# A four-layer hybrid trunk: HGRN2's first two decay levels in one tiled series, attention's value products for two blocks at a time, queries turned two heads at once

## The chip, the cores and the metric

The kernel runs on one core of one Trainium2 chip. The metric is the device time of one execution in microseconds, given as the median of several runs. The engines are named as the profile names them: PE (matrix products), PEld (its weight loads), DVE (vector engine), ACT (scalar engine), POOL, and SP (which here only issues transfers).

## The reference, cut to what matters

Four layers over 1024 positions of width 1024, all in float32. Layers 0 and 3 are HGRN2, layer 1 is sliding-window attention, layer 2 is gated DeltaNet. Each layer normalizes x, applies a shift and scale from the conditioning, projects, mixes over time, projects back and adds to x under a gate. The change touches the mixing of the HGRN2 layers and of the attention layer:

```python
def step(S, inp):                       # HGRN2, per chunk of 64 and per head; d = 128
    q_, k_, v_, lf = inp
    b = jnp.cumsum(lf, axis=-2)
    diff = b[..., :, None, :] - b[..., None, :, :]
    dec = jnp.exp(jnp.where(causal[:, :, None], diff, -jnp.inf))
    A = jnp.einsum('bhtd,bhsd,bhtsd->bhts', q_, k_, dec)
    o = jnp.einsum('bhts,bhse->bhte', A, v_) + jnp.einsum('bhtd,bhde->bhte', q_ * jnp.exp(b), S)
    ...
# attention: 16 query heads of 64 in 4 groups, 4 key heads, blocks of 128 queries, window 128
s = jnp.einsum('bnqhgd,bnkhd->bnhgqk', qb, kb) * (SW_DH ** -0.5)      # 128 queries x 256 keys
m = jnp.maximum(jnp.max(s, axis=-1, keepdims=True), sink)
p = jnp.exp(s - m)
p = p / (jnp.sum(p, axis=-1, keepdims=True) + jnp.exp(sink - m))
o = jnp.einsum('bnhgqk,bnkhd->bnqhgd', p, vb)
```

The HGRN2 matrix A has a different decay for each of the 128 channels, so it isn't one matrix product of q and k: the decays have to be multiplied into q and k relative to some position that lies between them.

## The kernel before

Activations lie with features on partitions and tokens in the free dimension, in two halves of 512 tokens (`hf`). Every projection is done in split float32: each operand is a high and a low part, and `mm3` (lines 354 to 359) issues three matmuls of 128x512 per 128 input features (high·high, high·low, low·high). Weights come by DMA as `w_raw`, and ACT and DVE split them into `w_hi` and `w_lo` (lines 328, 329, and 331, 332 with a scale). A projection's result lies in one of three PSUM banks (`proj_ps`) until ACT and DVE have evacuated it.

A layer's work is written as generators that yield after each piece of matmul work. `weave` runs several of them side by side: in a head of HGRN2 the mixing of head h (`mix`), the projections of head h+1, and a side stream that prepares the next layer's modulation. The final order of the instructions in each engine's queue is not left to that: the table `ORDER` holds for each of PE, ACT, DVE, SP and POOL a compressed list of places, and `in_order` (line 165) ties every instruction to the one before it in that list. The lists come from a planner that ran ahead of time. An engine works through its queue strictly in that order.

**HGRN2 mixing** (`hgrn2`, from line 1156; `mix` from line 1245), per layer, head and half, which makes 2 x 8 x 2 = 32 units. A is built in levels of growing distance, in groups of 4 sub-blocks of j = 2, 8 and 32 tokens (l = 1, 3, 5); level 0 (neighbours) is done beside level 1 with operands that the evacuation of the projection made (`q` of 48 columns a group, `k0`). At each level, ACT copies and DVE products build `X`, the decayed queries (lines 1281 to 1283). Then `products` (lines 1254 to 1263) multiplies `X` with `kg`, the decayed keys: 16 small matmuls, each with a stationary operand of 128x32 and a moving one of 128x48, four side by side in the four column groups of the array, so that outputs land in 32-partition strips of a `lev_ps` bank. A float32 product is two instructions in the profile. `tied` (line 284) makes such a set one unbroken series in PE's queue. At level 1 the series has two operand pairs, `(X, kg)` and `(q, k0)`; at level 3 one. DVE writes the wanted entries into `A` with masked copies (lines 1290 to 1296), and then q, k and the decays F are scaled for the next level (lines 1315 to 1321; line 1319 overwrites `kg`). Level 5 has 16 products of another shape (line 1305). Then `kg` is turned (line 1327, `kh_ps`), and the outputs and states follow chunk by chunk (lines 1337 to 1350). Buffers of a tag are reused in turn; `bufs` (line 1164) gives their number.

**Attention mixing** (`swa`, from line 1496; `mix` from line 1605), per group of 4 query heads and block of 128 queries: 4 x 8 = 32 blocks. Four transposes of 64 columns turn the queries (line 1616, `qt_ps`), two ACT casts write the high part to both halves of `qhi` (lines 1619, 1620), one DVE subtraction the low part (line 1621). Per head, a band mask and two products give the scores `s_ps` (lines 1631 to 1633). After the softmax, probabilities are turned (line 1654), and line 1660 multiplies them with the values: 128x64 stationary, 128x256 moving, two side by side in the two column halves of the array, for each of the two key blocks (only one for the first block of the sequence), as one tied series. Line 1666 multiplies the result by the gate.

The output projection of HGRN2 reads the mixed heads 0 to 6 back from DRAM (`out_load`, line 1450, issued on POOL's queue) into three buffers of a pool of their own (lines 1409, 1410, 1416). `rope_tables` (line 489) makes the rotary tables during the first layer.

Of the kernel before, what the change touches and what calls it, by code (L numbers as in the profile page):

```python
# [34 lines left out]
SB = {"q": 2, "tmp": 4, "qhi": 2, "pth": 2, "sm": 2, "zs": 2, "of": 3}  # L35
# [16 lines left out]
        "c-rk->2n;#6@S{DJ!ZAit|VJ4OSaH`?dm=)S+<3YkYfWfKCz7xCm2i;QjnqwaHyErmJdv>0-N9jVoX&a<f0Oj4<-pDA5ul7@*$O~<XgVvU&w"  # L52
        "dzj-J_`-r1d9A4!qQuSzq$-90ni@4bHS_3Nils1Q(v0768;0tE{prQBkUuo;m9m>VEWF_H-CF*`f!6!m-Ux>_nG5b1OxMdfHTYDK8vei&d4q"
        "7MNcMDxJGVFixXgKiz~1b{pJ!hk%Auj=S{*FXmW+Mx~Zf>zi7>!AgjVI4FzK?WLOEv$hCsP_)&6nq0-fRk{hsj2B)6O_c0a7&o=t(^#f({IK"
        "=O$}ByHg*9tH!GGKklHZ>-8a!?D_3Q+;MN2KSqWg<c&V>1>w%E~<a=&3Q24HK1FCu%z7YWD1*-<k58Q>I`*Q{cxpgW}G#?yAXg^~yyrk2@k%"
        "v{~BZZG`62d<Oe=G&_sj;!^*ROwM0OsehX=%yr^}d1p^Zy7y!7%@7KyUlAf#Sk&0-l3spXDMJoI1wy!J_mvc^+;LlqA;y(BhFrFjS;3FRx~^"
        "Rur(s1^x|p5LE_Lb((?d*X)nFpJzx<wgvz@g%LddFjVp4_97Avd)^*5;1~(Iv&Dcq5S?FdP>Vqp0oXc)LgiDft*y<hN~eqT^>1*gg~*tVF@j"
        "71hrTWVRY)?jY$2juRJ}P5Y8HY*wE=Kz>CQH_!5mAqNiNrrmPxj70DJ^l^C=v1`M%n69SjjdYkdGhp@dp))waFXfbsIA0Tw6(IHJ@DLbr_HQ"
        "WR?4glPE-R}ld!DOQb*g^DH`Ws6A*!h&!-9!ds4oVgILpRi0KVD<YfeoK8Zf?NuPB0`&(E=pdRvJ?@Gx0FH<NrfOy43YyV;B^BFekz4J166D"
        "ls*n(^!%*S3OMOStEWfr`{C^YxTm!xW@?8V|-~74(_|L=f_anA#<NWLD>Rf7j;qZb4hvX%kLPTl>Ncb8uZ%n+9Qs%BulnZ@a4Gp(AuZf6>P7"  # L60
        "{%ih#&lxiVtpPRKprnmA2neeq)P|1xl2F>iWq)t3LTxmE+Qm+&NU@9YtLSm65zt5F0^X@)g=V@(M5Qs^LOo;q^&MsE|hx?vKZwQ8iB@zJ&;K"
# [1740 lines left out]
```

## Time and profile before

| | |
|---|---|
| median of 3 runs | 2592.4 us (2590.6 to 2597.68) |
| profiled execution | 2594.64 us, span 2592.9 us |
| mean granted TensorE clock | 0.991 |
| PE busy | 2538.1 us, 98% of the span, 18271 matmuls |
| PEld busy | 2061.2 us, 79% |
| DVE busy | 2044.0 us, 79% |
| ACT busy | 1328.4 us, 51% |
| POOL busy | 158.9 us, 6% |
| DMA | 312.06 MB in 393618 packets, mean 120 GB/s |

The first HGRN2 layer lies at about 60 to 600 us of the span, attention up to about 1060, DeltaNet up to about 2060, the second HGRN2 layer behind it. In rows of the profile "128\*32" behind a matmul means 128 rows and 32 columns of the array; the tile sizes after it are those of the moving operand or of the result; "x64" counts instructions. A matmul's own length overlaps with the next matmul's: what a matmul takes from the queue is the distance between the starts.

### The profile page before, as it was taken

To read this page: it belongs to the slowest core of one execution; us is meant where nothing else is said; L and a number is where in the kernel's file an instruction comes from. 1 tells how busy PE (TensorE), PEld (TensorE's weight loads), DVE (VectorE), ACT (ScalarE), POOL (GpSimd) and SP (SyncE) were. 2 spreads that over 40 slices of the span, in tenths; PEclk is the share of its full clock that TensorE was granted. 3 is DMA by queue.
4 is the path that set the end of the run, shared out by engine and by line. 5 is a ranking of instruction groups with operands and counts; after the bars stand their busy time and mean duration, and the time that the engine had idled before them with its cause. 6 is when DMAs were issued, how large, how long until landed. Compare 5 with 4: busy or idle time off the path is not lost.

```text
span 2592.9 us, 50817 instructions
## 1 busy us (share of the span) xinstructions
PE 2538.1 (98%) x18271; PEld 2061.2 (79%) x18271; DVE 2044.0 (79%) x5663; ACT 1328.4 (51%) x3480; POOL 158.9 (6%) x382
## 2 busy tenths in 40 slices
PE   8999999999999999999999999999999999999999
PEld 4777777788888867787887788788788878888887
DVE  6586788887788888778998999898777847478885
ACT  5344344543465656455666666666544534344452
POOL 0000000001000000100001101110212000000000
PEclk9999999999999999999999999999999999999999
DMA  8233443644233253434344344333576412122453
GB/s 292 85 115 83 143 135 119 192 130 151 58 94 98 87 162 103 140 107 113 96 123 114 87 124 117 82 95 90 179 229 206 130 30 89 55 86 67 129 160 119
DMA packets 393618, 312.06 MB, mean 120 GB/s; under 512 B 74980, under 2 KB 320151, under 8 KB 393367
## 3 DMA queue, kind: packets, MB, share of 16 engines
q1 hardware_dynamic: 380822, 267.92, 35.5%
q0 software_dynamic: 12544, 40.90, 4.9%
q8 instruction: 144, 2.36, 0.4%
q14 instruction: 108, 0.88, 0.1%
HBM read 247.84 MB, written 60.88 MB: 119 GB/s over the span
## 4 chain that ended last, share of the span: by engine, by line
PE 83%; DMA 7%; DVE 4%; ACT 2%; issue 1%; SPq 1%; POOL 0%; DVEq 0%; ACTq 0%; POOLq 0%
PE proj_ps L357 12%; PE proj_ps L358 12%; PE proj_ps L359 12%; PE outp_ps L358 5%; PE outp_ps L359 5%; PE outp_ps L357 5%; PE projw_ps L358 2%; PE projw_ps L357 2%; PE projw_ps L359 2%; PE projt_ps L358 2%; PE projt_ps L357 2%; DMA ada_w<-in_ada_w_dram 2%; PE projt_ps L359 2%; PE lev_ps L1260 2%; DMA w_raw<-in_hg_in_w_dram 1%
## 5 line engine op out<-in xcount | busy, mean ns | idle before, releaser
L357 PE MATMUL proj_ps<-hhi,w_hi 128*128 128x512 f32 x1664 | 677.6, 408 | 3.1 <-ACT gd_tb L831 2.9
L358 PE MATMUL proj_ps<-hlo,w_hi 128*128 128x512 f32 x1664 | 675.6, 406 | 0.0
L359 PE MATMUL proj_ps<-hhi,w_lo 128*128 128x512 f32 x1664 | 672.6, 405 | 0.0
L357 PEld LDWEIGHTS proj_ps<-hhi,w_hi 128*128 128x128 f32 x1664 | 315.3, 190 | 62.7 <-ACT gd_tb L831 4.9
L359 PEld LDWEIGHTS proj_ps<-hhi,w_lo 128*128 128x128 f32 x1664 | 315.1, 189 | 58.1 <-issue 1.5
L358 PEld LDWEIGHTS proj_ps<-hlo,w_hi 128*128 128x128 f32 x1664 | 315.5, 190 | 56.3 <-issue 1.3
L328 ACT CAST w_hi<-w_raw 128x512 fp32r<-128x512 f32 x356 | 216.5, 610 | 233.3 <-PE proj_ps L358 109.7
L329 DVE TENSOR_TENSOR w_lo<-w_raw,w_hi 128x512 fp32r<-128x512 f32 x356 | 237.9, 674 | 99.6 <-ACT w_hi L328 97.5
L358 PE MATMUL outp_ps<-o_lo,w_hi 128*128 128x512 f32 x576 | 229.0, 398 | 0.7 <-DVE o_lo L1466 0.7
L357 PE MATMUL outp_ps<-o_hi,w_hi 128*128 128x512 f32 x576 | 228.0, 398 | 0.0
L359 PE MATMUL outp_ps<-o_hi,w_lo 128*128 128x512 f32 x576 | 227.7, 396 | 0.0
L331 ACT ACTIVATE w_hi<-w_raw,par 128x512 fp32r<-128x512 f32 (+1 forms) x136 | 94.7, 698 | 132.2 <-PE outp_ps L358 76.4
L833 DVE SCALAR_TENSOR_TENSOR gd_tb<-gd_xs,taps,gd_tb 128x512 f32<-128x512 f32 x192 | 145.2, 756 | 10.2 <-ACT gd_tb L831 8.8
L583 DVE SCALAR_TENSOR_TENSOR ada_acc<-ada_w,par,ada_acc 128x512 f32<-128x512 f32 x154 | 115.0, 747 | 30.4 <-DMA ada_w<-in_ada_w_dram 29.9
L332 DVE SCALAR_TENSOR_TENSOR w_lo<-w_raw,par,w_hi 128x512 fp32r<-128x512 f32 (+1 forms) x136 | 96.3, 715 | 43.9 <-ACT w_hi L331 43.3
L358 PEld LDWEIGHTS outp_ps<-o_lo,w_hi 128*128 128x128 f32 x576 | 108.7, 189 | 24.3 <-DVE o_lo L1466 2.9
L359 PEld LDWEIGHTS outp_ps<-o_hi,w_lo 128*128 128x128 f32 x576 | 108.5, 188 | 22.6 <-issue 1.8
L357 PEld LDWEIGHTS outp_ps<-o_hi,w_hi 128*128 128x128 f32 x576 | 108.6, 189 | 22.1 <-issue 1.2
L1457 POOL DMA_DIRECT2D o_in<-od x72 | 38.9, 540 | 1179.5 <-DVE sw_q L1540 319.3
L358 PE MATMUL projw_ps<-w_lo,hhi 128*128 128x512 f32 x256 | 102.5, 402 | 0.0
L357 PE MATMUL projw_ps<-w_hi,hhi 128*128 128x512 f32 x256 | 101.6, 401 | 0.9 <-ACT w_hi L328 0.9
L359 PE MATMUL projw_ps<-w_hi,hlo 128*128 128x512 f32 x256 | 101.9, 400 | 0.0
(432 smaller groups left out, 5394.5 us busy)
## 6 DMA issues: line engine op xcount, KB each, us to landing
ada_w<-in_ada_w_dram SPq DMA_DIRECT2D x160, 256.0 KB, 2.8
w_raw<-in_hg_in_w_dram SPq DMA_DIRECT2D x148, 256.0 KB, 2.9
w_raw<-in_gd_in_w_dram SPq DMA_DIRECT2D x128, 256.0 KB, 3.0
o_in<-od POOLq DMA_DIRECT2D x72, 256.0 KB, 3.7
x<-xd SPq DMA_DIRECT2D x64, 256.0 KB, 5.6
w_raw<-in_gd_out_w_dram SPq DMA_DIRECT2D x64, 256.0 KB, 3.1
...
```

What stands on the lines that cost most here:

```text
L328: nc.scalar.copy(hi, raw)
L329: nc.vector.tensor_tensor(lo, raw, hi.bitcast(F32), ALU.subtract)
L331: nc.scalar.activation(hi, raw, AF.Copy, scale=scale)
L332: nc.vector.scalar_tensor_tensor(lo, raw, scale, hi.bitcast(F32), ALU.mult, ALU.subtract)
L357: mm(out, a[0], b[0], start=start, stop=False)
L358: mm(out, a[0], b[1], start=False, stop=False)
L359: mm(out, a[1], b[0], start=False, stop=stop)
L583: self.step = self.nc.vector.scalar_tensor_tensor(acc, w, c, acc, ALU.mult, ALU.add)
L833: last = nc.vector.scalar_tensor_tensor(y, xs[:, j:j + HT], w(j), y, ALU.mult, ALU.add)
L1260: return nc.tensor.matmul(pl[gs, n, c * 48:(c + 1) * 48], k[:, c * P + g * 32:c * P + (g + 1) * 32], x[:, 4 * c + g, :], start=True, stop= ...
L1457: nc.gpsimd.dma_start(t, od[(k0 + k) * P:(k0 + k + 1) * P, sl])
```

## The change

1. **HGRN2, levels 1 and 3.** `products` takes three operand pairs, the two of level 1 and the one of level 3, and issues 48 products (96 instructions) as one tied series at level 3, into two `lev_ps` banks. At level 1 nothing is multiplied on PE. `X` of level 1 has a tile of its own (`hg_X1`), `kg` of level 1 stays as it is until the series, and the scaled keys of level 3 and later are written into the tile that held `f`; the quarter of them that isn't scaled is copied there by ACT. All masked copies into `A` come behind the series. Buffers: q 2 in the first HGRN2 layer (3 in the second, as before), f 3 (was 2), kg 2 (was 3), F 1 (was 2).
2. **Attention, value products.** They are issued once for two blocks of queries, as one tied series of up to 16 instructions into a whole PSUM bank; one DVE product of 512 columns then applies the gate. `pth` has 4 buffers (was 2).
3. **Attention, queries.** Two transposes of 128 columns turn two heads each; the second head of each pair comes out on partitions 64 to 127. Four ACT casts and two DVE subtractions of half the width write `qhi` and `qlo`.
4. **Smaller.** The rotary tables use two tiles fewer. The HGRN2 output load uses the four high weight buffers of `hgrn2`'s own pool in place of a pool of three.
5. **Order.** All five lists of `ORDER` are new (left out below).

```diff
--- before.py
+++ after.py
@@ -34,3 +34,3 @@
 GB = {"k": 5, "q": 4, "kt": 4, "v": 4, "tmp": 2, "tb": 4, "of": 2, "f256": 4, "ot": 1}
-SB = {"q": 2, "tmp": 4, "qhi": 2, "pth": 2, "sm": 2, "zs": 2, "of": 3}
+SB = {"q": 2, "tmp": 4, "qhi": 2, "pth": 4, "sm": 2, "zs": 2, "of": 3}
@@ -493,3 +489,3 @@
         pi = sp.tile([8, P], I32, name="pos_i", tag="pos_i", bufs=1)
-        pf = sp.tile([8, P], F32, name="pos_f", tag="pos_f", bufs=1)
+        pf = pi.bitcast(F32)
         nc.sync.dma_start(pi, ins["positions"].rearrange("o (n p) -> (o n) p", p=P))
@@ -542,3 +538,3 @@
                     gg = gb[:, a if w == 0 else 1 - a, :][:, None, :].to_broadcast([P, 8, 32])
-                    t = tmp("cg")
+                    t = tmp("rev")
                     if w == 1 and a == 0:
@@ -1163,3 +1159,3 @@
         H, HA, NG = 8, 7, 4 * NC
-        bufs = {"X": 1, "q": 3, "f": 2, "kg": 3, "qf": 3, "tmp": 3, "zs": 4, "kht": 1, "k0": 2}
+        bufs = {"q": 3 if i else 2, "f": 3, "kg": 2, "qf": 3, "tmp": 3, "zs": 4, "kht": 1, "k0": 2}
@@ -1213,3 +1209,3 @@
-        tl("zs"), tl("kht"), mp.tile([P, NC * 7 * 32], F32, name="hg_X", tag="hg_X", bufs=bufs["X"])
+        tl("zs"), tl("kht"), mp.tile([P, NC * 7 * 32], F32, name="hg_X", tag="hg_X", bufs=1)
@@ -1255,3 +1251,4 @@
-                    pl = self.psum("lev", "lev_ps", 2)[:, :192 * len(xks)].rearrange("p (n t) -> p n t", t=192)
+                    pa, pb = (self.psum("lev", "lev_ps", 2)[:, :192 * n].rearrange("p (n t) -> p n t", t=192) for n in (2, 1))
+                    pls = (pa[:, 0], pa[:, 1], pb[:, 0])
@@ -1259,9 +1256,9 @@
                         (x, k), gs = xks[n], slice(g * 32, (g + 1) * 32)
-                        return nc.tensor.matmul(pl[gs, n, c * 48:(c + 1) * 48], k[:, c * P + g * 32:c * P + (g + 1) * 32], x[:, 4 * c + g, :], start=True, stop=True)
+                        return nc.tensor.matmul(pls[n][gs, c * 48:(c + 1) * 48], k[:, c * P + g * 32:c * P + (g + 1) * 32], x[:, 4 * c + g, :], start=True, stop=True)
-                    self.tied([lambda n=n, c=c, g=g: mm(n, c, g) for n in range(len(xks)) for c in range(NC) for g in range(4)])
-                    return pl
+                    self.tied([lambda n=n, c=c, g=g: mm(n, c, g) for n in range(3) for c in range(NC) for g in range(4)])
+                    return pls
                 fv = f.rearrange("p (n b) -> p n b", b=2)
-                F = mp.tile([P, HT // 2], F32, name="hg_F", tag="hg_F", bufs=2)
+                F = mp.tile([P, HT // 2], F32, name="hg_F", tag="hg_F", bufs=1)
                 nc.vector.tensor_tensor(F, fv[:, :, 0], fv[:, :, 1], ALU.mult)
@@ -1278,3 +1275,3 @@
                     nx = 7 if j == 32 else 6
-                    X = mp.tile([P, NC * 7 * 32], F32, name="hg_X", tag="hg_X", bufs=bufs["X"])[:, :nq * nx * j]
+                    X = mp.tile([P, NC * (6 if l == 1 else 7) * 32], F32, name="hg_X", tag="hg_X1" if l == 1 else "hg_X", bufs=1)[:, :nq * nx * j]
                     xv = X.rearrange("p (n b j) -> p n b j", b=nx, j=j)
@@ -1283,16 +1280,19 @@
                     nc.vector.tensor_tensor(xv[:, :, nx - 1, :], xv[:, :, 4, :], bc(1, 2, 1)[:, :, 0, :], ALU.mult)
-                    if j < 32:
-                        xg = X.rearrange("p (g t) -> p g t", g=NG)
-                        pl = products((xg, kg), (q, k0)) if l == 1 else products((xg, kg))
-                        if l == 1:
-
-                            pv = pl[:, 1].rearrange("p (c t) -> p c t", c=NC)
-                            nc.vector.tensor_tensor(A.rearrange("p (c t) -> p c t", c=NC), pv[:, :, :32], self.eye32.rearrange("p (c t) -> p c t", c=NC), ALU.mult)
-                            av = A.rearrange("p (c n b) -> p c n b", c=NC, b=2)[:, :, :, 1]
-                            nc.vector.copy_predicated(av, self.lmask[0, 1].rearrange("p (c n) b j -> p c (n b j)", c=NC), pv[:, :, 32:])
-                        pv = pl[:, 0].rearrange("p (n b j) -> p n b j", b=6, j=j)
-                        av = A.rearrange("p (n b j) -> p n b j", b=4, j=j)
-                        for n, b0 in ((1, 0), (2, 3), (3, 5)):
-                            nc.vector.copy_predicated(av[:, :, n:, :], self.lmask[l, n], pv[:, :, b0:b0 + 4 - n, :])
-                        yield 700
+                    if l == 1:
+                        x1, k1 = X.rearrange("p (g t) -> p g t", g=NG), kg
+                        kg = f
+                        kn = kg.rearrange("p (n b j) -> p n b j", b=4, j=j)
+                        nc.scalar.copy(kn[:, :, 3, :], kv[:, :, 3, :])
+                    elif l == 3:
+                        pls = products((x1, k1), (q, k0), (X.rearrange("p (g t) -> p g t", g=NG), kg))
+                        pv = pls[1].rearrange("p (c t) -> p c t", c=NC)
+                        nc.vector.tensor_tensor(A.rearrange("p (c t) -> p c t", c=NC), pv[:, :, :32], self.eye32.rearrange("p (c t) -> p c t", c=NC), ALU.mult)
+                        av = A.rearrange("p (c n b) -> p c n b", c=NC, b=2)[:, :, :, 1]
+                        nc.vector.copy_predicated(av, self.lmask[0, 1].rearrange("p (c n) b j -> p c (n b j)", c=NC), pv[:, :, 32:])
+                        for m, pl in ((1, pls[0]), (3, pls[2])):
+                            pv = pl.rearrange("p (n b j) -> p n b j", b=6, j=1 << m)
+                            av = A.rearrange("p (n b j) -> p n b j", b=4, j=1 << m)
+                            for n, b0 in ((1, 0), (2, 3), (3, 5)):
+                                nc.vector.copy_predicated(av[:, :, n:, :], self.lmask[m, n], pv[:, :, b0:b0 + 4 - n, :])
+                        yield 1400
                     else:
@@ -1318,3 +1318,3 @@
                     nc.vector.tensor_tensor(qv[:, :, 2:4, :], xv[:, :, 3::nx - 4, :], bc(0, 1, 2), ALU.mult)
-                    nc.vector.tensor_tensor(kv[:, :, 0:3, :], kv[:, :, 0:3, :], bc(1, 4, 3), ALU.mult)
+                    nc.vector.tensor_tensor((kn if l == 1 else kv)[:, :, 0:3, :], kv[:, :, 0:3, :], bc(1, 4, 3), ALU.mult)
                     Fn = mp.tile([P, nq], F32, name="hg_F", tag=f"hg_F{l}", bufs=2)
@@ -1408,4 +1408,2 @@
             rst.close()
-        ost = ExitStack()
-        op = ost.enter_context(self.tc.tile_pool(name=f"hgo{i}", bufs=1, reuse_waits="tile"))
         for hf in range(2):
@@ -1415,3 +1413,3 @@
             if hf == 0:
-                ld = [self.out_load(od, 0, HA, x, op, "o_in", 3) for x in range(2)]
+                ld = [self.out_load(od, 0, HA, x, mp, "whi", WB) for x in range(2)]
                 p7 = lambda x: proj(H - 1, ds[H - 1], x, (1,))
@@ -1419,3 +1417,2 @@
             weave(self.tc, (mix(H - 1, ds[H - 1], (hf,)), 9250, 0, SPH, PRH), (a, tot, 0, 1, 0), (self.late, KT, 0, 0.8, 0))
-            ost.close()
             yield self.rest(i, w_out, range(HA, H), [ds[h]["o", hf] for h in range(HA, H)], hf, on)
@@ -1613,10 +1610,14 @@
                 pt = self.psum("tr", "qt_ps", 1)
-                for h in range(4):
-                    o = nn * 256 + h * 64
-                    nc.tensor.transpose(pt[:64, h * P:(h + 1) * P], d["q"][hf][:, o:o + 64], self.ident)
-                yield 436
+                for h in range(2):
+                    o = nn * 256 + h * P
+                    nc.tensor.transpose(pt[:, h * P:(h + 1) * P], d["q"][hf][:, o:o + P], self.ident)
+                yield 218
                 qhi, qlo = tl("qhi", F32R), qls[n % 2]
-                nc.scalar.copy(qhi[:64], pt[:64])
-                nc.scalar.copy(qhi[64:], pt[:64])
-                nc.vector.tensor_tensor(qlo[:64], pt[:64], qhi[:64].bitcast(F32), ALU.subtract)
+                qh, ql = (x.rearrange("p (m a t) -> p a m t", m=2, a=2) for x in (qhi, qlo))
+                p2 = pt[:, :256].rearrange("p (m t) -> p m t", m=2)
+                for a in range(2):
+                    s_ = slice(a * 64, a * 64 + 64)
+                    nc.scalar.copy(qh[s_, a], p2[s_])
+                    nc.scalar.copy(qh[64 - a * 64:P - a * 64, a], p2[s_])
+                    nc.vector.tensor_tensor(ql[:64, a], p2[s_], qh[s_, a].bitcast(F32), ALU.subtract)
                 rq = d["rq"][hf][:, nn * 4:nn * 4 + 4]
@@ -1648,4 +1649,5 @@
                     nc.vector.tensor_scalar(sm[:, h, :nk], sm[:, h, :nk], den[:, h:h + 1], None, ALU.mult)
-                po = self.psum("o", "pv_ps", 1)[:, :256].rearrange("p (m t) -> p m t", m=2)
-                nkb, p4s = nk // P, []
+                if nn % 2 == 0:
+                    po, p4s = self.psum("o", "pv_ps", 1).rearrange("p (m a t) -> p m a t", m=2, a=2), []
+                nkb = nk // P
                 for b in range(nkb):
@@ -1657,11 +1659,12 @@
                     nc.scalar.copy(ph, pt)
-                    p4s.append(ph.rearrange("p (m a t) -> p m a t", m=2, a=2))
-
-                self.tied([lambda b=b, a=a: nc.tensor.matmul(po[a * 64:(a + 1) * 64], vg[:, n + 1 - nkb + b, :], p4s[b][:, :, a, :], start=b == nkb - 1, stop=b == 0)
-                           for b in reversed(range(nkb)) for a in range(2)])
-                yield 860 * nkb
-                cs = slice(nn * P, (nn + 1) * P)
+                    p4s.append((n % 2, n + 1 - nkb + b, b == nkb - 1, b == 0, ph.rearrange("p (m a t) -> p m a t", m=2, a=2)))
                 if nn == 0:
                     of = tl("of", n=2 * HT).rearrange("p (m t) -> p m t", m=2)
-                nc.vector.tensor_tensor(of[:, :, cs], po, d["zs"][hf][:, :, cs], ALU.mult)
+                if nn % 2 == 0:
+                    continue
+                self.tied([lambda n2=n2, b=b, s0=s0, s1=s1, p4=p4, a=a: nc.tensor.matmul(po[a * 64:(a + 1) * 64, :, n2, :], vg[:, b, :], p4[:, :, a, :], start=s0, stop=s1)
+                           for n2, b, s0, s1, p4 in sorted(p4s, key=lambda z: (z[0], -z[1])) for a in range(2)])
+                yield 860 * len(p4s)
+                cs = slice((nn - 1) * P, (nn + 1) * P)
+                nc.vector.tensor_tensor(of[:, :, cs], po.rearrange("p m a t -> p m (a t)"), d["zs"][hf][:, :, cs], ALU.mult)
                 if nn == 3 and g == G - 1:
```

More of the change, by code (lines that the diff above doesn't have):

```diff
@@ L51 @@
     "PE": (
[L52 to L61, printed above, removed]
@@ new lines @@
+        "f0oYURAGrhCg9mxTb;;WjTQO{+&&pCbi^hI71@!A2XLI4RNAP_eULgw_(^&@l@L^`vbyO2a8krC7&sRo3esG}s>(h_|r8jaF*I9wC1ri)0#&"
+        "mZ)7JYb=*u@S%BkV;wdLIvs|SR->i61q-W`GZR=uhO@=x<1$FLZA~mpdB8D1hhdb#GwTqg63w3K@&7W1JsME7Pt(T;1}>VKGS@)8MfqSup_#"
+        "2rSA>71jq(3X=;KlXlYTO>DS=Q-3Xnh@z}>X=`^2aDk^p$AaqMsQs=6|9fK~ZP&kD<Yc83ye%50LfEvRq8odA`0IRdkB|CZYq%NtNnr<MCoR"
+        "FEP^>=1r52nZEUw?H;;X7kv^f4~j!h+2EqlWE=|K*aBdi}e`mPYUf{2W$S`4TTwp3q)-6M9p;4-W>vpDnpoG#=3iN*En`!MJ87!pnNS24Aq("
+        "-DXLKneDw>!zj;f#W4JSt|JytbOkY&fY0y8I{BzxhS%%t+(W9{i6C_5j)EL3|9E}=9Vsn_ZgJn_^?JV@X*D#&ihWx^xHmtTrU!gJtbV;qNaR"
@@ new lines @@
+        "=}78@daXDjl@sQcv-QTHjbOq0@DM{!A9N$oh|cZq|@N`4>9Afo`Ps$1it8u+Lc1w_3S5e<MsgrlUz2G?XOOR;gew6EugorsG~3yND|J_KVqi"
+        "Sn3c*d_Ry*YrBrvqM!1KWTcE7z`t5vm{jk3@Gz9RV*y8OYCopcGk?aB6>M@?V=_lJ!}+&l4WJFDXIw80sTAJmI~HV;8T}W?nvI&fNud)fesi"
+        "YP+MD@m$n_H3+lDVNPX3a8D&5^C6=8x7$mptFSMYF(8^U`zr%WEO`R?sv(q&9sJjmFTWPjiDlO*BWb%=GH^z9KmM3HRo(07$&C><Fg!PwO{("
+        "F?J?mof44|-}O;JzwbqXwhJhAJua*foxY_>=kqqr7dgNv`HY#<d%3Ya1JD*Ve9XZrUEXj=<*T=EesfY`pIzk3=4L7HMNRrhW}xg^O^Zv?!lO"
+        "_+kUD!Bs?L-?{}i5$lt8;MV|)jLhj1rw!!BjT=}zxONBsK63_MNSsb+K-<?}=T0EG;=$!9I0?_gkJLB>QFpLFx3DboS2i|O{`+vJ@cJVX{j("
@@ new lines @@
+        "Psk^%$p*=MTOa15S;CmrN*0I~jk2o^6cURZqPz4vg41qTrj!!7;A&CMAJ{_ztAFV3AicmDi&HHd>p5z9Lteh4s+(Dm~2@(Zsm({qa!9w(kB9"
+        "K6K|=0zs&Jbs7Og!^*{z*jWxyLa*n9{SO<w{L$W9>00>?%liMh5PqaaXu%L{sQ1Pzm0zK$){hfuYdgI`bWQCw-oqYq*!KuyH3{gmuqBoY&!+"
+        "Y_^sQw@7=yDsnFG3Q5SE$C5CG2uzDF@f1SFySJ%#7eB<odvs=BdsQ_RF9)lxrSpKzuEK43(XBdy${#4Tk(lyvZZ)RdbIt$SauHu0nCm6K5lT"
+        "%DSJUl~DjL4%270x@21H&XXtmm4$v)N~!vHnI1Sz1~eA0JPRjm@XB`|Z#pOG}WCf$WSxY*@@w_4iLA>=1iK#4uxS?%}kf7<6+;F?i9_(<5ho"
+        "l#>J>M(`de>gmOcFTG?9V5cDmQ!vXD4Aa(*S(}1U7Gs-Pq2EU2d{lxnF<21;otIy>&s@&c@2lTiKU)vj$mizhF*RTq8{<iitw||LOdyFW2KC"
@@ new lines @@
+    "SP": (
+        "c-o~@+iu%13?*ermSo4S5y#2AElbj(Db|-_@B55l4}I8%{r^AgkhbG2S=Rw0kcj5xh$4^VTyU1yFd1VFQAW`4gJKv9WsjffO04%D|CR`=a}K"
+        "JtqQPf0eG)HXjDTmXfXGdwNI;-GM^ssAcwQ8A=}UtL>g@4B4WmzXnH*A(deX_a>HT)+``sbk4hD^QcXz)%?jF2<(6FJnS0u}_3(NEOFJGU({"
+        "rLH}tQUd#O!V{2zTF+TKdkSW_y1Jd40=<uF<EA<j02-V)fh?$RmJS7gV;!AuE7f`X*K5-h4w$zb-h}xs6RQH&UH4l-IfW1kF++UqZSP0F~<Q"
+        "AUrWR{&3gSiWn!#^87Z}f16HQ0B5c3J@ot6|$jFc>;ab!mP*Rkg6SBdMLb6N}dVvnij=2!pgfM_CUP6hHwG@HLX(2Fq4wQhtN$0FkJLw!IPU"
+        "F-uHe+=vLC&gSXfqRbUa$kn&A9*rd306LIZ8FLWI~ZsNex=f2tr{_g4SJBA?c|Qo(xTy#N#*^3c_2lZ$^$ZC)&kOi^cVAZd)ss<<P<)RF^8s"
+        "a#OxRV-t6=iWHaPV!i$UCElm$I_fil-ALY^6WN{1$D2X(wHN*gZHj`Xhk#zQK%?n>>E6EoaJS#!IQvud@sq#(czk;FPviBwsuk@(Q{|=O%Qr"
+        "yV%=8OX%^7F"),
```

176 lines of the change are left out of this document (80 added, 96 removed).

## The prediction

> **What bounds the kernel now.** I read the page's busy table and its chain, then busy time by stage, then what the matmul queue waited for, then the matmul timeline around each kind of series that the change touches.
>
> ```profile
> PE 2538.1 (98%) x18271; PEld 2061.2 (79%) x18271; DVE 2044.0 (79%) x5663; ACT 1328.4 (51%) x3480; POOL 158.9 (6%) x382
> ...
> PE 83%; DMA 7%; DVE 4%; ACT 2%; issue 1%; SPq 1%; POOL 0%; DVEq 0%; ACTq 0%; POOLq 0%
> ```
>
> TensorE is busy for 2538.1 of 2592.9 us and carries 83% of the chain that ended last. Only 54.8 us are without a matmul in flight. The next table has, per window, its length, then busy us of PE, weight loads, DVE, ACT and POOL. The windows are the first HGRN2 layer, attention (two), DeltaNet, and the second HGRN2 layer, without their ends.
>
> ```profile
> 66.00:470.00 404.00, 395.19 (x3530) 315.65 (x3529) 303.60 (x961) 168.59 (x439) 8.89 (x11) 1.00 0.40 117
> 670.00:940.00 270.00, 266.08 (x1839) 223.62 (x1838) 223.44 (x657) 155.25 (x403) 4.85 (x9) 0.99 0.34 104
> 940.00:1065.00 125.00, 123.08 (x626) 93.97 (x625) 103.38 (x242) 71.30 (x163) 13.15 (x30) 0.99 0.37 115
> 1065.00:2010.00 945.00, 928.04 (x6088) 759.01 (x6087) 808.73 (x2139) 561.21 (x1649) 99.50 (x236) 0.99 0.46 126
> 2060.00:2480.00 420.00, 419.99 (x3782) 340.25 (x3781) 285.11 (x956) 180.19 (x476) 2.70 (x5) 1.00 0.27 82
> ```
>
> Each touched stage is a full matmul queue: 8.8 us idle in the first HGRN2 layer, 5.8 in attention, nothing in the second HGRN2 layer. So a step's price is the matmul time that it takes out of the queue, as long as no new wait opens. Busy time doesn't give that, because matmuls overlap; start-to-start times do. The waits of the matmul queue that bear on the change (us in total, times, longest):
>
> ```profile
> PE o_ps L1337 <- ACT hg_tmp L1350: 4.0, 3, 2.7
> ...
> PE lev_ps L1260 <- DVE hg_X L1283: 1.6, 3, 1.2
> ...
> PE s_ps L1632 <- ACT sw_qhi L1620: 1.3, 1, 1.3
> ```
>
> **The change, part by part.**
>
> **1. Levels 1 and 3 in one series.** Before, each of 32 (layer, head, half) units issues 64 matmuls at level 1 (16 products, two operands, two instructions each) and 32 at level 3. First level 1 alone, between projections, then level 3 alone (start, length):
>
> ```profile
> 2076.53 0.40 PE L359 MATMUL projw_ps<-w_hi,hlo 128*128 128x512 f32 x1
> 2076.85 0.55 PE L1260 MATMUL lev_ps<-hg_X,hg_kg 128*32 128x48 f32 x32
> 2077.22 0.52 PE L1260 MATMUL lev_ps<-hg_q,hg_k 128*32 128x48 f32 x32
> 2077.67 0.50 PE L357 MATMUL projw_ps<-w_hi,hhi 128*128 128x512 f32 x1
> 2078.00 0.39 PE L358 MATMUL projw_ps<-w_lo,hhi 128*128 128x512 f32 x1
> 2078.23 0.40 PE L359 MATMUL projw_ps<-w_hi,hlo 128*128 128x512 f32 x1
> ```
> ```profile
> 512.51 0.39 PE L357 MATMUL outp_ps<-o_hi,w_hi 128*128 128x512 f32 x1
> 512.82 0.55 PE L1260 MATMUL lev_ps<-hg_X,hg_kg 128*32 128x48 f32 x32
> 513.30 0.50 PE L358 MATMUL outp_ps<-o_lo,w_hi 128*128 128x512 f32 x1
> 513.64 0.40 PE L359 MATMUL outp_ps<-o_hi,w_lo 128*128 128x512 f32 x1
> ```
>
> A wide matmul's pitch is 0.23 us (2078.00 to 2078.23). The one ahead of a series takes 0.32, and the first behind it 0.33: entering and leaving a 128*32 series costs about 0.1 us at each neighbour, besides the last products' run-out. Whole cost: level 1, 2078.00 - 2076.53 - 2 x 0.23 = 1.01; level 3, 513.64 - 512.51 - 0.46 = 0.67. So 32 more matmuls inside a series cost 1.01 - 0.67 = 0.34, and in the merged series level 3 costs 0.34 instead of 0.67. Saved 0.33 x 32 = **10.6 us**. If only the two neighbours' delays go, it is 0.2 x 32 = 6.4. I take 10.6, since the step from the first operand to the second (2077.22) shows no pause.
>
> What it costs elsewhere: a ScalarE copy of the unscaled quarter of the keys into the tile that held f (128x128, 32 times; rows in part 3: between 272 ns for 128x128 and 427 for 128x256, I take 0.30, 9.6 us), on an engine busy for 168.6 of 404 us. Nothing if so; if the DVE product behind it became the last thing waited for, 0.3 a unit. Against that, level 1's scaling of the keys no longer waits until the products have read them, because it writes to another tile. Later instead: the three masked copies of level 1 and the diagonal's two stand behind level 3 on DVE, and q, kg and k0 are held until the merged series. First-layer q goes from 3 buffers to 2, kg from 3 to 2, f from 2 to 3. The queue orders are written for this; what it may cost is the first rival. F with one buffer has readers and writer on DVE alone, in order: nothing.
>
> **2. Value products of two blocks in one series** (16 pairs in place of 32 series). Eight, then four instructions alone:
>
> ```profile
> 1027.77 0.40 PE L358 MATMUL outp_ps<-o_lo,w_hi 128*128 128x512 f32 x1
> 1028.10 1.08 PE L1660 MATMUL pv_ps<-sw_pth,v 128*64 128x256 f32 x8
> 1029.11 0.50 PE L359 MATMUL outp_ps<-o_hi,w_lo 128*128 128x512 f32 x1
> 1029.44 0.39 PE L357 MATMUL outp_ps<-o_hi,w_hi 128*128 128x512 f32 x1
> ```
> ```profile
> 943.58 0.65 PE L1660 MATMUL pv_ps<-sw_pth,v 128*64 128x256 f32 x4
> 944.16 0.50 PE L357 MATMUL outp_ps<-o_hi,w_hi 128*128 128x512 f32 x1
> ```
>
> Eight cost 1029.44 - 1027.77 - 0.46 = 1.21. To the next start, eight take 1.01 and four 0.58, so four more take 0.43 and eight more 0.86. Saved 1.21 - 0.86 = 0.35 x 16 = **5.6 us** (0.2 x 16 = 3.2 with the neighbours' delays alone). The first block's products wait for the second's softmax; pth has four buffers in place of two for that, and po a whole bank. Behind the last pair the gating product is 512 wide instead of 256, at most 0.26 us more in two tails (part 3's rows); the rest of the output projection covers it.
>
> **3. Queries turned two heads at once.** Four transposes of 64 columns become two of 128. Before, next to 128-column transposes, and four of those alone:
>
> ```profile
> 941.30 0.38 PE L1654 MATMUL pt_ps<-ident,sw_sm 128*128 128x128 f32 x2
> 941.51 0.60 PE L1616 MATMUL qt_ps<-ident,sw_q 128*64 128x128 f32 x4
> 941.87 0.47 PE L357 MATMUL outp_ps<-o_hi,w_hi 128*128 128x512 f32 x1
> 942.18 0.39 PE L358 MATMUL outp_ps<-o_lo,w_hi 128*128 128x512 f32 x1
> ```
> ```profile
> 485.38 0.39 PE L358 MATMUL proj_ps<-hlo,w_hi 128*128 128x512 f32 x1
> 485.61 0.60 PE L1327 MATMUL kh_ps<-ident,hg_kg 128*128 128x128 f32 x4
> 485.96 0.48 PE L359 MATMUL proj_ps<-hhi,w_lo 128*128 128x512 f32 x1
> 486.28 0.39 PE L357 MATMUL proj_ps<-hhi,w_hi 128*128 128x512 f32 x1
> ```
>
> Two 128-column transposes take 0.21 (941.30 to 941.51). Four narrow ones take 0.36 to the next start, four wide ones 0.35: width is free, so two fewer save 0.21 x 32 = **6.7 us**. The other engines pay:
>
> ```profile
> L1619 ACT CAST sw_qhi<-qt_ps 64x512 fp32r<-64x512 f32 x32 | 18.6, 580 | 28.7 <-PE qt_ps L1616 27.6 <-PE s_ps L1632 1.0
> L1620 ACT CAST sw_qhi<-qt_ps 64x512 fp32r<-64x512 f32 x32 | 18.5, 578 | 0.4
> L1311 ACT COPY hg_at<-lev_ps 32x256 f32<-32x256 f32 x64 | 23.2, 362 | 21.5 <-PE lev_ps L1305 20.9
> L1188 ACT COPY hg_kg<-hg_k 128x256 f32<-128x256 f32 x32 | 13.7, 427 | 3.7 <-DVE hg_k L1185 3.2
> L1228 ACT COPY hg_v<-projw_ps 128x128 f32<-128x128 f32 x16 | 4.4, 272 | 0.0
> L1621 DVE TENSOR_TENSOR sw_qlo<-qt_ps,sw_qhi 64x512 fp32r<-64x512 f32 x32 | 21.7, 677 | 5.2 <-ACT sw_qhi L1620 5.0
> L1666 DVE TENSOR_TENSOR sw_of<-pv_ps,sw_zs 128x256 f32<-128x256 f32 x32 | 13.4, 420 | 6.1 <-PE pv_ps L1660 6.0
> ```
>
> Four casts of 64x256 lie between the 362 and 427 ns of the 256-wide rows; at 0.40 they take 1.60 in place of 1.16, so 0.44 x 32 = 14 us more of ScalarE, busy for 226.6 of 395 us here. Two subtractions at 420 in place of one at 677: 5.2 us more of DVE, less 16 x (2 x 420 - 677) = 2.6 from part 2, on 326.8 of 395. Both have room, but the first score matmul stands 0.44 us later behind its transposes. That was waited for once (1.3 us). If every block paid, 14 us; I take **+1.0**, by the single wait.
>
> The Trainium skill, "TensorEngine Tiling (Array Packing)", Key Properties, says that a change of tiling mode drains TensorE. For the series of parts 1 and 2 that is what their neighbours' delays show. Applied to the 128*64 transposes as well, it would add a saving of up to 0.35 x 32 = 11 us, an estimate by part 2's price; but 0.36 against 0.35 us shows no drain there, and the sum goes by the rows.
>
> **4. The rest.** Rope: two tiles fewer, their writers and readers in order on DVE or behind the same DMA as before: nothing. The late HGRN2 output load takes four weight buffers, idle by then, in place of a pool of three, on POOL's queue, which is busy for 8.9 of 404 us; projections of the last head cover it. Planned anew: decoding the tables, PE has 14166 places for 14230 (64 transposes fewer), ACT 3048 for 2952, DVE 5679 for 5663, SP 1353 and POOL 378 as before. In the DeltaNet part about 85% of PE's neighbours, 74% of DVE's and 73% of ACT's are the old ones: mended there, new around the changed layers, SP's loads and their buffers with it. I take idle time as unchanged.
>
> **Sum.** -10.6 - 5.6 - 6.7 + 1.0 = -21.9. The profiled execution took 2594.6 (span 2592.9), 2.2 above the median of three, 2592.4. So 2572.7 for such a run and 2570.5 for the median: **2570**, own range 2563 to 2577.
>
> **Rivals.**
> - *Held buffers open waits in the first HGRN2 layer* (14%). A projection's evacuation for the next head needs the q tile that the other half's merged series still reads, and a full PSUM bank then stops TensorE. For it: two q tiles are all that two halves need, and a head's mixing overlaps the next head's projection. Against: three PSUM banks of slack. Price: the layer's idle 8.8 us doubled, 2579; at most seven heads x the longest wait of 2.7, 19 us, 2589.
> - *The merged series is waited for: slower* (4%). PE is in order, so a series that stands in its queue before level 3's X is ready holds every projection behind it. It eats the gain at 21.9/32 = 0.68 us a unit, and is slower by over 0.3% (7.8 us, about the least that can be told from no change) from 0.93: 2601 at 0.95. Against: such waits now come to 1.6 us in all.
> - *The merging doesn't do it* (5%): ends of series cost the same wherever they lie, for instance at the change of PSUM tile inside; transposes alone remain: 2592.4 - 6.7 = 2586.
> - *The new order fills better* (13%): the first HGRN2 layer gets as dense as the second, 8.8 us less: 2561.
> - *The narrow transposes' ends go too* (4%): another 11 us, 2559.
>
> **Numbers.** 60% for the forecast. Faster by over 0.3% (below 2584.6): forecast, fuller order, narrow ends, and most of the held buffers, 0.87. Same: the unmerged case and the worst of the held buffers, 0.09. Slower: 0.04. The range 2556 to 2584 takes in the single prices' low ends (4.2 + 2.4 less saved) and a score wait paid in every second block.
>
> **What would show it.** lev_ps of levels 1 and 3 as one series of 96 with about 1.35 us of cost; pv_ps as series of 16 with 2.07; 64 qt_ps transposes of 128 columns; PE idle near 55 us. I am wrong if lev_ps waits on hg_X grow past a few us, if hg_q evacuations stall proj_ps between 66 and 470 us, or if 96 cost 1.7.

## The result, and the profile after

The changed kernel takes 2576.15 us in the median (2572.48 to 2579.39, 4 runs), the kernel before 2593.93 us beside it (2590.6 to 2597.68, 4 runs): ratio 0.994, 95% interval 0.9917 to 0.9963. Timed once more, unaltered, it took 2572.34 us against 2591.6, ratio 0.9919 (0.9898 to 0.994). So the change is worth some 18 us (15.6 and 21.0 by the two ratios); the forecast was 2570 with an own range of 2563 to 2577. The profiled execution took 2572.48 us with a span of 2570.8.

The busy and chain rows of the page after:

```profile
PE 2512.7 (98%) x18207; PEld 2044.4 (80%) x18207; DVE 2059.3 (80%) x5679; ACT 1347.7 (52%) x3574; POOL 164.0 (6%) x382
...
PE 61%; DVE 6%; DMA 3%; ACT 1%; issue 1%; SPq 0%; POOL 0%; DVEq 0%; POOLq 0%; ACTq 0%
```

The chain (second row) could be followed back only to 681 us of the span here, so its shares add up to 72% and don't compare with those of before. TensorE lost 25.4 us of busy time and the span 22.1; time without a matmul in flight went from 54.8 to 58.1 us. The matmul timeline, at places with one touched series between projections, answers to those of the prediction: the merged levels, a series of twelve value products and one of sixteen, and two query transposes.

```profile
2058.02 0.40 PE L355 MATMUL projw_ps<-w_hi,hlo 128*128 128x512 f32 x1
2058.35 0.55 PE L1257 MATMUL lev_ps<-hg_X,hg_kg 128*32 128x48 f32 x32
2058.71 0.52 PE L1257 MATMUL lev_ps<-hg_q,hg_k 128*32 128x48 f32 x32
2059.05 0.54 PE L1257 MATMUL lev_ps<-hg_X,hg_f 128*32 128x48 f32 x32
2059.52 0.50 PE L353 MATMUL projw_ps<-w_hi,hhi 128*128 128x512 f32 x1
2059.86 0.39 PE L354 MATMUL projw_ps<-w_lo,hhi 128*128 128x512 f32 x1
...
942.43 1.59 PE L1665 MATMUL pv_ps<-sw_pth,v 128*64 128x256 f32 x12
943.96 0.50 PE L354 MATMUL outp_ps<-o_lo,w_hi 128*128 128x512 f32 x1
...
736.36 1.95 PE L1665 MATMUL pv_ps<-sw_pth,v 128*64 128x256 f32 x16
738.24 0.39 PE L353 MATMUL projt_ps<-w_hi,hhi 128*128 128x256 f32 x1
...
827.51 0.39 PE L353 MATMUL proj_ps<-hhi,w_hi 128*128 128x512 f32 x1
827.74 0.40 PE L1613 MATMUL qt_ps<-ident,sw_q 128*128 128x128 f32 x2
827.89 0.48 PE L354 MATMUL proj_ps<-hlo,w_hi 128*128 128x512 f32 x1
828.21 0.39 PE L355 MATMUL proj_ps<-hhi,w_lo 128*128 128x512 f32 x1
```

Read as in the prediction: 96 level products cost 2059.86 - 2058.02 - 0.46 = 1.38 us (forecast about 1.35). Twelve value products take 1.53 to the next start, sixteen 1.88 (forecast 1.01 + 0.86 = 1.87). Two transposes take 0.15 to the next start where four took 0.36: 0.21 saved, as forecast. All three queue prices came out.

Waits of the matmul queue that bear on the change (us in total, times, longest):

```profile
PE ada_row L563 <- DMA ada_w<-in_ada_w_dram: 4.8, 1, 4.8
...
PE s_ps L1633 <- ACT sw_qhi L1621: 3.0, 1, 3.0
...
PE projw_ps L353 <- DVE hg_q L1172: 2.0, 1, 2.0
...
PE lev_ps L1257 <- DVE hg_X L1280: 1.0, 3, 0.5
```

No wait opened at the merged levels (1.0 us, 1.6 before). The projection that waited 2.0 us for `hg_q` stands at 61.6 us of the span, ahead of the first merged series (77.9 us): `hg_q` is there what empties a projection's bank, not a tile that is held. New is the wait for a modulation weight at the beginning; the wait for the queries' casts, once, at attention's end, was 1.3 us before.

Where the time went, by stage. The next table is worked out from the traces: a stage runs from one share of the projections' matmuls, counted by the columns that they move, to another (first layer with the beginning from the first matmul up to 20%, attention 25 to 40%, DeltaNet 40 to 67.5%, second HGRN2 layer 77.5 to 95%; what lies between isn't shown). "Queue" and "rest" split attention: queue is what its matmuls take when each distance of two starts is put at the lower quartile of the same pair of neighbours over all traces; rest is what is left, waits and half clock among it. The level of "queue" depends on how neighbours are paired, so only its differences are used: other pairings put the 10.1 us between before and after at 9 to 15.

| kernel | median us | before beside it | ratio (95%) | begin + first HGRN2 | attention | queue + rest | DeltaNet | second HGRN2 |
|---|---|---|---|---|---|---|---|---|
| before | 2593.93 | | | 523.2 | 430.5 | 412.9 + 17.6 | 793.2 | 414.3 |
| after | 2576.15 | 2593.93 | 0.994 (0.9917 to 0.9963) | 517.8 | 426.4 | 402.8 + 23.7 | 779.5 | 409.5 |
| after_again | 2572.34 | 2591.6 | 0.9919 (0.9898 to 0.994) | 517.6 | 426.9 | 402.8 + 24.1 | 780.4 | 410.1 |
| lev_split | 2582.62 | 2591.6 | 0.996 (0.9948 to 0.9971) | 523.9 | 426.3 | 402.8 + 23.5 | 784.8 | 415.3 |
| pv_split | 2579.27 | 2591.6 | 0.995 (0.9933 to 0.9968) | 516.7 | 432.7 | 408.0 + 24.7 | 782.1 | 409.9 |
| q_undone | 2585.38 | 2591.6 | 0.9975 (0.9962 to 0.9987) | 519.6 | 435.7 | 410.5 + 25.2 | 786.8 | 409.5 |
| before_new_dn | 2589.64 | 2593.46 | 0.9985 (0.9972 to 0.9998) | 524.5 | 430.6 | 412.9 + 17.6 | 788.9 | 413.8 |
| b_qp | 2593.63 | 2593.46 | 1.0002 (0.9989 to 1.0015) | 521.5 | 433.5 | 403.9 + 29.6 | 785.6 | 414.5 |
| before_q | 2592.11 | 2595.67 | 0.9991 (0.9977 to 1.0006) | 525.8 | 429.1 | 407.0 + 22.1 | 788.7 | 414.9 |
| part1_alone | 2579.48 | 2591.63 | 0.9957 (0.9942 to 0.9973) | 519.1 | 427.2 | 412.9 + 14.3 | 785.9 | 409.8 |
| c_at | 2577.37 | 2593.46 | 0.9941 (0.9921 to 0.996) | 517.0 | 427.5 | 403.9 + 23.6 | 783.6 | 409.9 |
| after_qorder | 2590.84 | 2593.46 | 0.9998 (0.9985 to 1.0012) | 516.8 | 445.0 | 402.8 + 42.2 | 784.0 | 409.6 |
| after_halves | 2580.27 | 2595.67 | 0.9937 (0.9918 to 0.9956) | 518.4 | 429.3 | 402.8 + 26.6 | 780.4 | 412.0 |
| after_start | 2579.05 | 2595.67 | 0.9932 (0.9912 to 0.9952) | 523.0 | 426.3 | 402.8 + 23.6 | 782.1 | 411.2 |

A stage's time is that of one execution: DeltaNet, with code and order unchanged, took 793.2, 788.7 and 785.6 us in before, before_q and b_qp. Nearly all of that spread is half clock: stretches with a granted clock of 0.5, counted at half their length, come to 13.7, 8.5 and 5.1 us there. A few us of one stage in one trace decide nothing; ratios do.

### The profile page after: what moved, and what is told of

It is laid out like the page before. It is cut to its first block, busy times and chain, and to the rows that moved or that the text cites. A ratio compares the mean times of both kernels' runs of the same rounds, so it can differ in the third digit from the quotient of the medians.

```text
span 2570.8 us, 50729 instructions
## 1 busy us (share of the span) xinstructions
PE 2512.7 (98%) x18207; PEld 2044.4 (80%) x18207; DVE 2059.3 (80%) x5679; ACT 1347.7 (52%) x3574; POOL 164.0 (6%) x382
## 4 chain that ended last, share of the span: by engine, by line
PE 61%; DVE 6%; DMA 3%; ACT 1%; issue 1%; SPq 0%; POOL 0%; DVEq 0%; POOLq 0%; ACTq 0%
PE proj_ps L353 9%; PE proj_ps L355 9%; PE proj_ps L354 9%; PE outp_ps L354 4%; PE outp_ps L353 4%; PE outp_ps L355 4%; PE projw_ps L355 1%; PE projw_ps L353 1%; PE projw_ps L354 1%; DVE gd_tb L829 1%; PE pt_ps L1656 1%; DMA ada_w<-in_ada_w_dram 1%; PE w_ps L1084 1%; PE pv_ps L1665 1%; PE w_ps L1100 1%
```

## Experiments

Diffs that hold no code put the edit in words.

**lev_split**: part 1's merging undone in the queue alone. In each of the 32 units one matmul is moved into the series.

```diff
-lev_ps x96 (level 1: 64, level 3: 32), next matmul
+lev_ps x64 (level 1), next matmul, lev_ps x32 (level 3)
```

> The changed kernel with one edit in TensorE's order list: in each of the 32 level series the matmul that followed the series (128 columns of the array) stands behind the first 64 of its 96 instructions. Theory A (each end of a 128x32 series costs its neighbours about 0.1 us and the run-out of the last products): 32 x 0.33 = 10.6 us slower than the changed kernel. Theory B (the ends cost nothing, the gain came from something else in the change): within 2 us of the changed kernel.

0.996 against 0.9919: 10.6 us slower by the ratios (10.3 by the medians). 6.3 us lie in the first HGRN2 layer, 5.2 in the second. The cut as the matmul timeline of this kernel shows it:

```profile
2066.07 0.40 PE L351 MATMUL projw_ps<-w_hi,hlo 128*128 128x512 f32 x1
2066.40 0.55 PE L1253 MATMUL lev_ps<-hg_X,hg_kg 128*32 128x48 f32 x32
2066.76 0.52 PE L1253 MATMUL lev_ps<-hg_q,hg_k 128*32 128x48 f32 x32
2067.22 0.50 PE L349 MATMUL projw_ps<-w_hi,hhi 128*128 128x512 f32 x1
2067.65 0.55 PE L1253 MATMUL lev_ps<-hg_X,hg_f 128*32 128x48 f32 x32
2068.13 0.50 PE L350 MATMUL projw_ps<-w_lo,hhi 128*128 128x512 f32 x1
2068.47 0.39 PE L351 MATMUL projw_ps<-w_hi,hlo 128*128 128x512 f32 x1
```

From 2066.07 to 2068.47 less three pitches of 0.23 is 1.71, against 1.38 uncut: 0.33 a unit. Part 1's price and its total, undone in the new order, are shown.

**pv_split**: the same for the 16 series of value products.

```diff
-pv_ps x16 (even block 8, odd block 8), next matmul
+pv_ps x8 (even block), next matmul, pv_ps x8 (odd block)
```

> The changed kernel with one edit in TensorE's order list: in each of the 16 value series the matmul that followed it stands between the two blocks' products. Theory A (as for the level series): 16 x 0.35 = 5.6 us slower than the changed kernel. Theory B (attention, which gained about 4 us where 11 were forecast, has slack in its matmul queue, so a saved series end there is given back as waiting): under 2 us slower.

0.995 against 0.9919, 8 us by the ratios and 6.9 by the medians; attention 5.8 us longer, 5.2 of it queue work (16 x 0.33). In attention the ends of a series cost what was said (5.6); the runs lost 1 to 2 us more.

**q_undone**: in the changed kernel, the queries turned as before.

```diff
-2 transposes of 128 columns, 4 casts of 64x256, 2 subtractions of 64x256
+4 transposes of 64 columns, 2 casts of 64x512, 1 subtraction of 64x512
```

> The changed kernel with the queries turned as before: four transposes of 64 columns in the places of the two, two casts of 64x512 in the places of the first two of four, one subtraction in place of two. Theory A (two transposes are 0.21 us of the matmul queue, the narrower casts are hidden): 32 x 0.21 = 6.7 us slower than the changed kernel. Theory B (four casts of 0.36 us in place of two of 0.58 delay the scores and eat the gain): within 2 us, or faster.

13.0 us slower by the medians, twice the price. Attention is 8.8 us longer than in after_again, 7.7 of it queue work (410.5 against 402.8), near the 6.7 forecast. Another 6.4 us lie in DeltaNet (786.8 against 780.4), whose instructions and order are the same and which has no more half clock (6.8 us, 8.5 in after_again): what stretches it isn't shown. Undoing a step in a planned order may measure more than the step. Hence the next runs do parts alone, on the old order.

**before_new_dn**: in the kernel before, DeltaNet in the new order on all queues, no instruction changed.

> The kernel before with one thing of the change: the DeltaNet layer's instructions (the same ones, in number and kind) issued on every queue in the order that the changed kernel gives them. Theory A, the new order of the DeltaNet layer is worth its 13 us by itself (793.2 us in the trace of before, 779.5 and 780.4 in two traces of the changed kernel): span 12 to 14 us shorter than before's, some 2578 us in time, with the DeltaNet layer at 779 to 782 us and all other stages within 1.5 us of before. Rival B, the gain comes from what precedes the layer (buffers and engines are handed over earlier by the cheaper attention): DeltaNet stays at 790 to 793 us, time within 3 us of before.

0.9985 (0.9972 to 0.9998), 3.9 us (0.5 to 7.3). Theory A falls on its size: the 13 us that two pairs of traces showed in DeltaNet are not the order's own. A few us are, and 5 to 7 are half clock: 13.7 us of it in before's DeltaNet, 6.8 and 8.5 in the changed kernel's two traces.

**b_qp**: in the kernel before, parts 2 and 3 alone, in the old order.

```diff
-qt_ps x4 narrow, 2 casts, 1 subtraction; pv_ps x8 at each block
+qt_ps x2 wide, 4 casts, 2 subtractions; pv_ps x16 at the odd block
```

> The kernel before, with its old order kept on all queues, and in it parts 2 and 3 of the change alone: the value products of a pair of blocks as one series at the odd block's place, and the queries turned two heads at once (both subtractions behind all four casts). HGRN2 and DeltaNet stay as before. Theory A, the changed kernel's new order of the attention layer eats what the edits bring: here the attention layer takes 416 to 420 us (430.5 in before, 426.4 in the changed kernel), and the time is 10 to 15 us under before. Rival B, the edits' own latency (casts and products that come later) eats it, whatever the order: attention takes 425 to 428 us here too, and the time is 3 to 6 us under before.

1.0002 (0.9989 to 1.0015): no gain at all, where the sum has 11.3 us (5.6 + 6.7 - 1.0) for these parts. Theory A falls, and B forecast too much. The queue work did fall, by 9.0 us, and the rest rose by 12.0. The waits of attention's matmuls on the softmax's engines between 640 and 930 us, first in the kernel before, then here:

```profile
PE s_ps L1632 <- ACT sw_qhi L1620: 1.3, 1, 1.3
PE s_ps L1633 <- DVE sw_qlo L1621: 0.4, 1, 0.4
```
```profile
PE s_ps L1633 <- ACT sw_sm L1645: 1.5, 4, 0.6
PE pt_ps L1657 <- ACT sw_pth L1660: 1.1, 2, 0.7
PE s_ps L1635 <- DVE sw_qlo L1623: 0.9, 1, 0.9
PE s_ps L1634 <- ACT sw_qhi L1620: 0.8, 1, 0.8
PE pt_ps L1657 <- DVE sw_sm L1650: 0.6, 2, 0.4
PE qt_ps L1612 <- DVE sw_qlo L1623: 0.3, 1, 0.3
```

Two waits of 1.7 us in all became eleven of 5.2, on exponentials, copies of the turned probabilities and casts: many small ones, spread over ScalarE and VectorE. Over the whole stage the time without a matmul rose from 5.8 to 14.0 us, and the loss by half clock from 3.4 to 6.8. The longest single wait, 3.3 us (1.6 before), is not of the softmax but of the next layer's modulation.

**before_q**: part 3 alone, in the old order.

> The kernel before, with its old order kept on all queues, and in it part 3 of the change alone: two transposes of 128 columns, four casts and two subtractions for each block instead of four, two and one, all at the old places. Parts 2 and 3 together on the old order gave nothing (2593.6 against 2593.5 us), though their queue work in the attention layer fell by 9 us. Theory A, it is the queries' casts: ScalarE has 0.3 us more for each block (four of 0.367 us for two of 0.58 us) and VectorE 0.16 us more (two of 0.418 us for one of 0.677 us), scores and their exponentials come later, and waits eat the shorter transposes and what part 2 brings: this kernel is 3 to 8 us slower than before, with attention at 434 to 438 us. Theory B, no part costs, but any shortening of TensorE's queue in an order that stays turns into waits for the softmax: this kernel is within 3 us of before.

0.9991 (0.9977 to 1.0006): a gain of 2.3 us, between a loss of 1.6 and a gain of 6.0. Theory A falls, since the longer casts make nothing slower. Queue work fell by 5.9 us and the rest rose by 4.5. Part 3's own sum, 6.7 - 1.0, is just inside the interval, and so is nothing.

**part1_alone**: the changed kernel with attention as in the kernel before, code and order, on all queues.

```diff
-parts 2 and 3, attention's new order
+attention's code and order of the kernel before
```

> The changed kernel with parts 2 and 3 both undone and the attention layer wholly as in the kernel before (its code, its instructions and their order on all queues); HGRN2's merged series and the changed kernel's orders of the beginning, of both HGRN2 layers and of DeltaNet stay. It tells what parts 2 and 3 are worth in the finished kernel when each attention layer has an order made for it. Theory A, nothing: shortening the attention layer's queue turned into waits there, as on the old order (parts 2 and 3 gave 0 there); ratio to before 0.993 to 0.995, some 2576 to 2580 us where before has 2593, with attention at 427 to 431 us. Theory B, they are worth the sum's 11 us or nearly: ratio to before 0.997 to 0.999, 2585 to 2590 us, with attention at 430 to 431 us and the other stages as in the changed kernel. Between these, 0.995 to 0.997, they are worth the 4 us that the attention layer shortened between the two traces.

0.9957 (0.9942 to 0.9973), a gain of 11.1 us over before (7.0 to 15.0). The ratio lies in the range named for the case between A and B: against the changed kernel's 0.994 and 0.9919, parts 2 and 3 with their order bring about 4 to 10 us in the finished kernel, by intervals that overlap, so neither nothing nor all of their 11.3 is excluded. In the trace attention itself gains almost nothing by them: 427.2 us without, 426.4 and 426.9 with, at 10.1 us less queue work. Waits take only a part of that back: the stage's time without a matmul is 4.7 us without them, 7.0 and 5.9 with them, its half clock 1.7 us against 1.7 and 5.1. What takes the rest, and where else the 4 to 10 us lie, isn't shown.

**c_at**: the changed kernel with attention's instructions put back in the old order; parts 2 and 3 stand at their old counterparts' places, both subtractions behind the four casts.

> The changed kernel with the old order of the attention layer put back on all queues, as far as the layer's instructions exist in both (the merged value series stand at the odd block's place, the two turned pairs and their four casts at the old one's place, both subtractions behind all four casts); HGRN2 and DeltaNet keep the changed kernel's order. Theory A (the new attention order is some 8 us worse than the old one): attention at 416 to 420 us against 426.4, time some 6 to 10 us under the changed kernel, 2562 to 2566 us, faster than both kernels. Rival B (the edits' latency, not the order): attention at 425 to 428 us, time within 2 us of the changed kernel. Should the old order at the hand-over from HGRN2 fit badly with the changed kernel's first layer, the first HGRN2 stage or its boundary grows by some us.

0.9941 (0.9921 to 0.996), the same as the changed kernel within the intervals; attention 427.5 us. Theory B: attention's new order is no worse than the old one, and no better that can be told. My reading of the two first traces, that the new order ate some 8 us, was wrong.

**after_qorder**: the first of a block's two subtractions moved behind all four casts.

```diff
                     nc.scalar.copy(qh[64 - a * 64:P - a * 64, a], p2[s_])
+                for a in range(2):
+                    s_ = slice(a * 64, a * 64 + 64)
                     nc.vector.tensor_tensor(ql[:64, a], p2[s_], qh[s_, a].bitcast(F32), ALU.subtract)
```

> The changed kernel with one move: of each block, the first of the two subtractions for the low parts of the queries stands directly ahead of the second, behind all four casts, on VectorE. In the changed kernel's trace ScalarE's third cast waits for VectorE's first subtraction (6.5 us over 7 such waits). Theory A, that wait is part of what attention lost: waits of a cast for a subtraction go away, attention falls by 2 to 5 us from 426.4 us and the time by as much. Rival B, the scores wait for the last of casts and subtractions anyway, and the first subtraction comes later now: attention within 2 us, time within 2 us of the changed kernel.

0.9998 (0.9985 to 1.0012): it gives nearly the whole change away, some 15 to 20 us, 18.6 of them in attention (445.0). Neither theory saw it. From this kernel's waits of the matmul queue:

```profile
PE s_ps L1631 <- DVE sw_qlo L1619: 15.7, 11, 2.9
```

VectorE works in order, and the second subtraction stands up to 21 places behind the first in its queue. Moved there, the first lets the scores that need it, and the projections behind them in TensorE's queue, stand for up to 2.9 us. One subtraction of 418 ns a block, in the wrong place, costs more than parts 2 and 3 bring. The wait of a cast for it was not the fault to mend.

**after_halves**: the turned heads stored so that what one cast writes lies together.

```diff
-                qh, ql = (x.rearrange("p (m a t) -> p a m t", m=2, a=2) for x in (qhi, qlo))
+                qh, ql = (x.rearrange("p (a m t) -> p a m t", m=2, a=2) for x in (qhi, qlo))
...
-                        hs = slice((2 * hp + h2) * P, (2 * hp + h2 + 1) * P)
+                        hs = slice((2 * h2 + hp) * P, (2 * h2 + hp + 1) * P)
```

> The changed kernel with the turned heads stored so that the two heads of one cast lie side by side (the tile's columns ordered by half, then pair) and not two columns' blocks apart; same instructions in the same order on all queues. The third cast then no longer overlaps in its columns with what the first subtraction reads, so that ScalarE does not wait for VectorE between the casts (6.5 us over 7 such waits in the changed kernel's trace). Theory A, that wait delays the scores: attention falls by 2 to 5 us from 426.4 us, the time by as much. Theory B, the scores wait for something else as late: within 2 us of the changed kernel; the wait of cast for subtraction is gone from ScalarE's list in either case.

0.9937 (0.9918 to 0.9956), no difference from the changed kernel. What both theories took for sure failed: the wait of the cast for the subtraction is still there. ScalarE's groups between 660 and 1040 us, the changed kernel's first and then this one's (busy us, mean ns, idle before and what ended it):

```profile
L1620 ACT CAST sw_qhi<-qt_ps 64x256 fp32r<-64x256 f32 x64 | 23.5, 367 | 26.7 <-PE qt_ps L1613 19.4 <-DVE sw_qlo L1622 6.5
L1621 ACT CAST sw_qhi<-qt_ps 64x256 fp32r<-64x256 f32 x64 | 23.4, 366 | 0.8
```
```profile
L1620 ACT CAST sw_qhi<-qt_ps 64x256 fp32r<-64x256 f32 x64 | 23.5, 368 | 28.0 <-PE qt_ps L1613 19.7 <-DVE sw_qlo L1622 7.6
```

6.5 us became 7.6, so interleaved columns are not its cause. What is stays open: cast and subtraction still read the same bank `qt_ps`, and neither that nor a tile for each half was tried.

**after_start**: the 659 instructions of the beginning in their old order.

> The changed kernel with the old order of its beginning put back on all queues: the 659 instructions ahead of the first HGRN2 layer's levels, which are the same in both kernels, stand in before's relative order. In the changed kernel TensorE stands 4.8 us for a table's load (ada_row for ada_w) before the first wide product, and the beginning takes 33.4 and 34.4 us against 29.5. Theory A, the new order of loads and rows at the beginning gives 4 us away: here the beginning takes 29 to 31 us and the time falls by 3 to 5 us. Rival B, what is late at the beginning is made up in the first HGRN2 layer (its weights arrive when they arrive): the layer grows by as much and the time stays within 2 us.

0.9932 (0.9912 to 0.9952), no difference. The beginning is 4.1 us shorter (29.3 against 33.4 us) and the first HGRN2 layer 9.3 longer (493.7 against 484.4, about 5 of them by half clock). Rival B: the first wide product's place in time is not what sets the layer's end. A stall that stands second in the list of waits (4.8 us on a load) was worth nothing that can be told.

None of these kernels beats the changed one beyond its interval.

## Why the prediction was right

- *Part 1, 10.6 us.* Right in price (0.33 a unit) and in total: 10.3 to 10.6 by undoing it; doing it, part1_alone less the DeltaNet order, gives 7.2, with a few us of doubt in each, and part1_alone's two HGRN2 stages are 8.6 us shorter than before's. Of the two rivals that feared it, a merged series that is waited for shows as three waits of 1.0 us in all, and held buffers as none that the list of waits tells. That merging doesn't do it is excluded by lev_split.
- *Parts 2 and 3, 11.3 us.* The queue prices held. The step that failed is "So a step's price is the matmul time that it takes out of the queue, as long as no new wait opens", with "Both have room" and the 1.0 us for a later score: on the old order waits did open, and with half clock they took 12.0 us where the queue gave 9.0 (b_qp). Shares of busy time (DVE 326.8 of 395 us) say nothing of a chain that goes through ScalarE and VectorE for each block. Alone they brought 0 (b_qp, loss of 3.9 to gain of 2.9), in the finished kernel about 4 to 10, and there waits and half clock explain only 2 to 5 of the 10 us that attention didn't gain. ScalarE's casts took 9.8 us more (46.9 for 37.1; forecast 14, at 0.40 where 0.367 was measured), VectorE's subtractions 5.1 more and the gating products 2.4 less, as forecast. How much of b_qp's waits comes from these longer casts and how much from TensorE being sooner at the same chain isn't settled: before_q has the casts alone and 4.5 us more of rest, part 2 adds 7.5.
- *Part 4, "I take idle time as unchanged".* 54.8 to 58.1 us in all, but not stage by stage. The DeltaNet order, taken as nothing, brings 3.9 us (0.5 to 7.3).
- *The sum.* 21.9 forecast, some 18 measured: part 1 as said, parts 2 and 3 short by a few us, an unforeseen 3.9 on the other side. Of the 18, up to some 6 us came through fewer half-clock stretches, an estimate from the mean clocks (last section), and no term of the prediction has them. That the total came so near is partly luck.
- *Narrow transposes' ends, 2559.* Excluded: undoing part 3 adds 7.7 us to attention's queue, about the two transposes' own time (6.7), not that plus 11. The rule of the Trainium skill, "TensorEngine Tiling (Array Packing)", Key Properties, that a change of mode drains TensorE, agrees with the 0.33 us for one more cut of a 128\*32 series (lev_split); for the 128\*64 transposes no run here shows it.
- *The new order fills better, 2561.* The beginning and the first HGRN2 layer together lost 5.4 us (523.2 to 517.8), part 1's half and no more.
